# A streaming-encoder layer: two of the four sums of the first modulation as one-row TensorE products, and V's first rounding on ScalarE

## The chip, the core and the metric

One core of a Trainium2 chip runs the whole layer as one program. The metric is the device time of that program in microseconds (us); the median of three runs of the kernel before is 1326.62 us. The engines are called by their short names: PE (TensorE), DVE (VectorE), ACT (ScalarE), POOL (GpSimd) and SP (SyncE, which here only issues transfers).

## What is computed

The layer takes x (1024 rows of 1024 values) and a conditioning vector c of 1024 values. What matters here is the beginning of the reference:

```
mod = jnp.dot(jax.nn.silu(c), w_ada[l]) + b_ada[l]
sh_a, sc_a, g_a, sh_m, sc_m, g_m = jnp.split(mod, N_MOD, axis=-1)
h = modulate(rmsnorm(x, g_attn_norm[l]), sh_a, sc_a)
proj = jnp.dot(h, w_in[l])
```

`modulate` is h * (1 + scale) + shift. Everything behind it (two kinds of attention, the output projection, a gated MLP) starts from `proj`, and so from the shift and the scale, each of them 1024 sums over the 1024 values of silu(c).

## The kernel before, in words

The channels are cut into eight blocks of 128 (number d, 0 to 7), which lie on the 128 partitions; x has eight row tiles x0 to x7 of 128 rows, and h = 0 or 1 names the first or second four of them.

**The modulation.** The weights of scale and shift are packed in four blocks (dd, 0 to 3). One block serves two channel blocks d, has 512 columns, and is loaded in four chunks of 512 KB (`adaw`, L209), each with two of the eight groups k of 128 input channels. There are five chunk buffers, so that a chunk of the next block is loaded when one of the last block has been used. `ada_pair(dd)` (L271) makes the sums on DVE: one `tensor_scalar` (L276) and seven `scalar_tensor_tensor` (L278), all 128 x 512, add k's weights times silu(c) into `adacc`. This leaves 128 partial sums for each column, one for each partition; PE adds them up with a vector of ones (`p_ada`, L293), which puts the 128 columns on 128 partitions. Three short DVE instructions (L296 to L298) then make the two columns of `modT` for this d, scale and shift.

**x.** SP loads x0 to x7 behind the four chunks of block 0. For each tile ACT squares it and sums the squares (L224), POOL makes the reciprocal root (L119, L120), and DVE multiplies the tile by it (L226).

**The stage around the change.** For each d PE transposes the eight 128 x 128 pieces of x (`ht_ps`, L233), four for each h. ACT (h = 0 and the rounded half of h = 1, L236, L239) and DVE (h = 1, L241) apply scale and shift on the way out of PSUM. Each product is computed with split operands: a rounded part (hi) and the rest (lo, L242 on POOL for h = 0 and on DVE for h = 1), and three matmuls of 256 columns (L154 hi x hi, L155 hi x lo, L156 lo x hi). So `qk` takes 24 matmuls for each d, 192 in all. The weights of `qk` are split too (L77 on ACT, L84 on POOL). From d = 4 on, two pieces of V's weights are split for each d (`wv0_split`, L261): the rounding by `hi_of` on DVE (L81), the rest on POOL (L84), and a sum of squares on DVE (L267).

**What sets the order.** The order in which the instructions stand on each engine is made by a scheduler with a timing model when the program is built; each engine then runs its list strictly in that order, and so does SP with its transfers. The code asks in some places that one instruction comes after another (`issue_after`).

Of the kernel before, what the change touches and what calls it, by code (L numbers as in the profile page):

```python
# [13 lines left out]
F32 = mybir.dt.float32  # L14
# [4 lines left out]
AF = mybir.ActivationFunctionType  # L19
# [5 lines left out]
P = 128  # L25
# [3 lines left out]
ND = D // P  # L29
# [35 lines left out]
def layer_kernel(ctx, tc, I, out):  # L65
    nc = tc.nc
    pe, act, dve, pool, sp = nc.tensor, nc.scalar, nc.vector, nc.gpsimd, nc.sync
# [7 lines left out]
    def hi_of(eng, o, i):  # L75
        if eng == "a":
            act.activation(o, i, AF.Copy)  # L77
        elif eng == "p":
            pool.tensor_scalar(o, i, 1.0, 0.0, op0=MUL, op1=ADD)
        else:  # L80
            dve.tensor_copy(o, i)  # L81

    def lo_of(eng, o, i, hi):
        (pool if eng == "p" else dve).tensor_tensor(o, i, f32(hi), op=SUB)  # L84
# [15 lines left out]
    ones = cst.tile([P, P], F32, name="ones")  # L100
# [4 lines left out]
    cs = cst.tile([P, ND], F32, name="cs")  # L105
# [28 lines left out]
    ps = psA.__enter__()  # L134
# [3 lines left out]
    def rtile(name, shape=(P, 512), dt=F32):  # L138
        return apg.tile(list(shape), dt, name=name, tag="R", bufs=4)
# [10 lines left out]
    def gemm3(pt, pairs, start=True, stop=True):  # L150

        n = len(pairs)
        for i, (sh, sl, mh, ml) in enumerate(pairs):
            pe.matmul(pt, sh, mh, start=(start and i == 0), stop=False)  # L154
            pe.matmul(pt, sh, ml, start=False, stop=False)  # L155
            last = pe.matmul(pt, sl, mh, start=False, stop=(stop and i == n - 1))  # L156
        anchor["pe"] = last.ins
# [47 lines left out]
    wada = {}  # L205

    def load_ada(dd, c):
        w = st.tile([P, 2, 512], F32, name=f"adaw_{dd}_{c}", tag="wa", bufs=5)
        anchor["ada"] = sp.dma_start(w[:], I["w_ada_a"][dd][:, 2 * c:2 * c + 2]).ins  # L209
        wada[dd, c] = w  # L210
# [18 lines left out]
    def mod_transpose(src, k, h, row, pspool, psum_tag, pb, hpool, tag, tmp, nbuf, veng, leng):  # L229

        pt = pspool.tile([P, 512], F32, name=f"ht_ps{row}_{k}_{h}", tag=psum_tag, bufs=pb)
        for j in range(4):
            pe.transpose(pt[:, j * P:(j + 1) * P], src(j), ident[:])  # L233
        pg = hpool.tile([P, 2, 512], F32R, name=f"hT{row}_{k}_{h}", tag=tag, bufs=nbuf)
        a, b = modT[:, row, k:k + 1], modT[:, row + 1, k:k + 1]
        anchor["act"] = act.activation(pg[:, 0], pt[:], AF.Identity, scale=a, bias=b).ins  # L236
        v = tmp.tile([P, 512], F32, name=f"hv{row}_{k}_{h}", tag="hv", bufs=2)
        if veng == "a":
            act.activation(v[:], pt[:], AF.Identity, scale=a, bias=b)  # L239
        else:  # L240
            dve.tensor_scalar(v[:], pt[:], a, b, op0=MUL, op1=ADD)  # L241
        lo = (dve if leng == "v" else pool).tensor_tensor(pg[:, 1], v[:], f32(pg[:, 0]), op=SUB)  # L242
        anchor["lo" + leng] = lo.ins
        return pg
# [4 lines left out]
    accs = {}  # L249
    ssw0 = cst.tile([P, ND], F32, name="ssw0")  # L250

    wv0, wv0r = [], []

    def wv0_load():
        with tc.issue_after(anchor["ada"]):
            for k in range(ND):
                r = st.tile([P, 256], F32, name=f"wv0_r{k}", tag="wvr", bufs=8)
                anchor["sp"] = sp.dma_start(r[:], I["w_v"][0][:, k, :]).ins
                wv0r.append(r)

    def wv0_split(k):  # L261
        w = hw.tile([P, 2, 256], F32R, name=f"wv0_s{k}", tag="ws", bufs=16)
        junk = st.tile([P, 512], F32, name=f"wv0_j{k}", tag="wvj", bufs=1)
        with tc.issue_after(anchor["lov"]), tc.issue_after(anchor["lop"]):
            hi_of("v", w[:, 0], wv0r[k][:])
            lo_of("p", w[:, 1], wv0r[k][:], w[:, 0])
            dve.tensor_tensor_reduce(junk[:, :256], wv0r[k][:], wv0r[k][:], 1.0, 0.0, MUL, ADD,  # L267
                                     accum_out=ssw0[:, k:k + 1])
        wv0.append((w[:, 0], w[:, 1]))

    def ada_pair(dd):  # L271
        acc = rtile(f"adacc_{dd}")
        for k in range(ND):
            w = wada[dd, k // 2][:, k % 2]
            if k == 0:
                dve.tensor_scalar(acc[:], w, cs[:, 0:1], None, op0=MUL)  # L276
            else:
                dve.scalar_tensor_tensor(acc[:], w, cs[:, k:k + 1], acc[:], op0=MUL, op1=ADD)  # L278
        accs[dd] = acc

    ada_pair(0)
    for d in range(ND):
        dd, half = divmod(d, 2)
        if half == 0 and dd + 1 < ND // 2:
            for c in range(4):
                load_ada(dd + 1, c)
            if dd + 2 == ND // 2:
                wv0_load()
            ada_pair(dd + 1)
        pt = ps.tile([P, 512], F32, name=f"p_ada{d}", tag="mm", bufs=2)  # L290
        for i in range(2):
            c0 = half * 256 + i * P
            pe.matmul(pt[:, i:i + 1], accs[dd][:, c0:c0 + P], ones[:, 0:1], start=True, stop=True)  # L293

        tmp = cst.tile([P, 1], F32, name=f"adat{d}", tag="adat", bufs=2)
        dve.tensor_scalar(tmp[:], pt[:, 0:1], pk[:, C_B + 8 + d:C_B + 9 + d], 1.0, op0=ADD, op1=ADD)  # L296
        dve.tensor_tensor(modT[:, 0, d:d + 1], tmp[:], pk[:, C_GA + d:C_GA + d + 1], op=MUL)
        dve.tensor_tensor(modT[:, 1, d:d + 1], pt[:, 1:2], pk[:, C_B + d:C_B + d + 1], op=ADD)  # L298
        for h in range(2):
            hT[d, h] = mod_transpose(lambda j: xs[4 * h + j][:, d * P:(d + 1) * P], d, h, 0, ps, ("T", "pv")[h], 1,  # L300
                                     hw, "hT", st, 16, "v" if h else "a", "v" if h else "p")
        if d >= ND // 2:
            for k in range(2 * d - ND, 2 * d - ND + 2):
                wv0_split(k)
        for t in range(NT):
            h, j = divmod(t, 4)
            sl = slice(j * P, (j + 1) * P)
            gemm3(qk0[h][:, j * 256:(j + 1) * 256],
                  [(hT[d, h][:, 0, sl], hT[d, h][:, 1, sl]) + wqk[d]], start=(d == 0 and j % 2 == 0), stop=(d == ND - 1 and j % 2 == 1))
# [717 lines left out]
    for n in range(len(tiles) + DEPTH):  # L1027
        if n < len(tiles):
            u, i = tiles[n]
# [3 lines left out]
            if i % 4 == 2 and n + 2 < len(tiles):  # L1033
                v = tiles[n + 2][0]
# [4 lines left out]
        if n >= DEPTH:  # L1039
            u, i = tiles[n - DEPTH]  # L1040
# [66 lines left out]
    def mt(tag, shape, name, dt=F32):  # L1107
        return mp["a" if tag in ("raw", "w2", "ws") else "b"].tile(list(shape), dt, name=name, tag=tag, bufs=MB[tag])
# [72 lines left out]
    for t in range(NT):  # L1181
        pt = ps2.tile([P, 1024], F32, name=f"op{t}", tag="op", bufs=3)
# [69 lines left out]
    c0 = mt("c", [P, 4, 512], "c0")  # L1252
# [385 lines left out]
def build(arrays):  # L1638
    nc = bacc.Bacc("TRN2", target_bir_lowering=False, num_devices=1, dynamic_dma_scratch_size=1024)
    I = {k: nc.dram_tensor(k, v.shape, mybir.dt.from_np(v.dtype), kind="ExternalInput").ap()  # L1640
         for k, v in arrays.items()}
    out = nc.dram_tensor("out_0_dram", (S, D), F32, kind="ExternalOutput").ap()
    with tile.TileContext(nc, schedule_with_timeline_sim=True) as tc, ExitStack() as ctx:
        layer_kernel(ctx, tc, I, out)
    return nc
# [8 lines left out]
```

## Time and profile before

| | us |
|---|---|
| three runs | 1329.13, 1322.44, 1326.62 |
| the profiled execution | 1326.91 |
| its span, first to last instruction | 1325.1 |
| PE, DVE, ACT, POOL busy in the span | 1191.0, 1086.5, 623.6, 580.7 |

The profiled execution took 1.8 us more than its span. Times in the views are microseconds from the span's start. A row of a timeline gives start, duration, engine, line, operation, the tiles written and read, the count, and in brackets how long the engine stood idle before it and what released it. The matmuls of a run overlap, so that the distance from start to start tells their rate, not their duration.

### The profile page before, as it was taken

The page shows a single profiled execution, that of the slowest core. Times are in us where ns is not written, and L with a number is a line of the kernel's source. Part 1 is how long each engine was busy: PE and PEld are TensorE (multiplying, and loading weights), DVE is VectorE, ACT ScalarE, POOL GpSimd, SP SyncE. Part 2 cuts the span into 40 slices and gives each one's busy share as a digit, 9 for nine tenths or more (in the row PEclk, how much of TensorE's full clock was granted, in tenths as well). Part 3 has the DMA queues.
Part 4 walks back from the last instruction along what each step waited for, and adds up shares of the span by engine and source line. Part 5 has one row for each costly group of instructions (what it writes and reads, how often), then busy time and mean ns, then how long its engine had stood idle before and what let it go on. Part 6 is the DMA issues. An engine that isn't in the chain of part 4 may idle for free.

```text
span 1325.1 us, 18721 instructions
## 1 busy us (share of the span) xinstructions
PE 1191.0 (90%) x6168; PEld 992.2 (75%) x6168; DVE 1086.5 (82%) x1928; ACT 623.6 (47%) x1132; POOL 580.7 (44%) x613
## 2 busy tenths in 40 slices
PE   3899899888678788878899999999999998999998
PEld 3789888878556577756677888888888886888886
DVE  6979989887699978774789888888889886687667
ACT  5454654364556444452476444443444444433331
POOL 5485773586567643344515445454444431000000
PEclk9899899999879898888999999999999998999999
DMA  8416769665124677679602333333243336943441
GB/s 323 144 55 149 169 146 198 154 166 121 28 80 80 150 162 140 139 153 324 260 16 80 127 104 133 114 109 126 94 133 104 128 103 243 394 135 116 128 160 63
DMA packets 223689, 190.57 MB, mean 144 GB/s; under 512 B 148708, under 2 KB 166884, under 8 KB 223592
## 3 DMA queue, kind: packets, MB, share of 16 engines
q1 hardware_dynamic: 223592, 189.38, 49.9%
q8 instruction: 48, 0.79, 0.2%
q14 instruction: 49, 0.40, 0.1%
HBM read 117.24 MB, written 37.49 MB: 117 GB/s over the span
## 4 chain that ended last, share of the span: by engine, by line
PE 50%; DVE 4%; DMA 3%; issue 2%; ACT 1%; POOL 1%; SPq 0%; POOLq 0%; DVEq 0%; ACTq 0%
PE p L1130 10%; PE p L1131 10%; PE p L1132 10%; PE dnA_P L1465 2%; PE dnA_P L1467 2%; PE dnA_P L1466 2%; DMA PTm<-hlm 2%; PE dnB_P L1467 2%; PE dnB_P L1465 2%; PE dnB_P L1466 2%; PE dnA L1465 1%; PE dnA L1466 1%; PE dnA L1467 1%; PE sm L803 1%; PE dnB L1467 1%
## 5 line engine op out<-in xcount | busy, mean ns | idle before, releaser
L77 ACT ACTIVATE dnP<-dnr 128x1024 fp32r<-128x1024 f32 x73 | 77.5, 1064 | 117.3 <-PE dnA_P L1467 46.3
L1439 DVE TENSOR_TENSOR dnP<-dnr,dnP 128x1024 fp32r<-128x1024 f32 x72 | 87.9, 1223 | 52.7 <-ACT dnP L77 52.7
L73 POOL TENSOR_SCALAR hlm<-Pm,rim 128x512 f16<-128x512 f32 (+2 forms) x96 | 68.8, 728 | 85.7 <-DVE rim L832 45.6
L84 POOL TENSOR_TENSOR wf<-wu,wf 128x512 fp32r<-128x512 f32 x22 | 38.7, 1758 | 116.2 <-ACT wf L77 116.2
L84 POOL TENSOR_TENSOR wb<-wu,wb 128x512 fp32r<-128x512 f32 x22 | 44.7, 2033 | 84.9 <-ACT wb L77 57.1
L1301 DVE SCALAR_TENSOR_TENSOR u<-c,cvp,u 128x1023 f32<-128x1023 f32 x44 | 55.8, 1309 | 27.8 <-ACT u L1300 23.7
L891 PE MATMUL pvm<-PTm,vt 128*128 128x256 f16 (+1 forms) x320 | 47.9, 302 | 27.1 <-DMA PTm<-hlm 27.0
L851 DVE SCALAR_TENSOR_TENSOR hlm<-Pm,rim,hlm 128x512 f16<-128x512 f32 (+2 forms) x96 | 66.3, 708 | 6.0 <-POOL hlm L73 5.8
L73 POOL TENSOR_SCALAR hlc<-Pc,ric 128x640 f16<-128x640 f32 (+2 forms) x64 | 48.8, 764 | 47.0 <-DVE ric L832 17.8
L829 ACT ACTIVATE Pc<-sc,mc 128x640 f32<-128x640 f32 (+2 forms) x64 | 42.2, 660 | 54.9 <-DVE mc L818 36.9
L891 PEld LDWEIGHTS <-vt 128*128 128x128 f16 x320 | 32.9, 111 | 42.3 <-issue 21.2
L829 ACT ACTIVATE Pm<-sm,mm 128x128 f32<-128x128 f32 (+3 forms) x64 | 47.2, 738 | 35.1 <-DVE sm L821 9.7
L1300 ACT ACTIVATE u<-c,cvp 128x1024 f32<-128x1024 f32 x44 | 52.3, 1238 | 23.6 <-DVE c L1399 16.5
L77 ACT ACTIVATE wc<-ws 128x512 fp32r<-128x512 f32 x21 | 13.3, 632 | 92.9 <-DVE ws L1149 87.1
L851 DVE SCALAR_TENSOR_TENSOR hlc<-Pc,ric,hlc 128x640 f16<-128x640 f32 (+2 forms) x64 | 50.9, 801 | 7.0 <-POOL hlc L73 6.8
L154 PE MATMUL ipq<-wq_s,hT 128*128 128x256 f32 x192 | 56.2, 293 | 0.0
L1302 DVE SCALAR_TENSOR_TENSOR u<-c,cvp,u 128x1022 f32<-128x1022 f32 x44 | 55.5, 1300 | 0.0
L155 PE MATMUL ipq<-wq_s,hT 128*128 128x256 f32 x192 | 55.0, 286 | 0.0
L156 PE MATMUL ipq<-wq_s,hT 128*128 128x256 f32 x192 | 54.9, 286 | 0.0
L1466 PE MATMUL dnA_P<-dnP 128*128 128x512 f32 x132 | 51.3, 389 | 0.0
L1467 PE MATMUL dnA_P<-dnP 128*128 128x512 f32 x132 | 51.3, 389 | 0.0
L1465 PE MATMUL dnA_P<-dnP 128*128 128x512 f32 x132 | 51.2, 389 | 0.0
(443 smaller groups left out, 4399.7 us busy)
## 6 DMA issues: line engine op xcount, KB each, us to landing
wu<-w_up SPq DMA_DIRECT2D x44, 512.0 KB, 3.5
dnr<-g_d SPq DMA_DIRECT2D x73, 256.0 KB, 2.7
aw<-w_ada SPq DMA_DIRECT2D x48, 256.0 KB, 3.3
g_d<-u SPq DMA_DIRECT2D x22, 512.0 KB, 2.8
dnr<-w_down SPq DMA_DIRECT2D x44, 256.0 KB, 5.4
adaw<-w_ada_a SPq DMA_DIRECT2D x16, 512.0 KB, 6.4
x<-x SPq DMA_DIRECT2D x16, 512.0 KB, 9.0
g_d<-gs SPq DMA_DIRECT2D x22, 256.0 KB, 2.7
```

The costliest lines, as they stand in the source:

```text
L73: pool.tensor_scalar(o, i, s, 1.0, op0=MUL, op1=MUL)
L77: act.activation(o, i, AF.Copy)
L84: (pool if eng == "p" else dve).tensor_tensor(o, i, f32(hi), op=SUB)
L829: act.activation(pr[:, :n], sv, AF.Exp, bias=m[:], scale=-1.0, accum_out=rsum[:, 0:1])
L851: dve.scalar_tensor_tensor(hl[:, w:2 * w], pp, ri[:], hl[:, :w], op0=MUL, op1=SUB)
L1130: pe.matmul(pt, sh, pg[:, 0], start=(k == 0 and not add), stop=False, skip_group_check=skip)
L1131: pe.matmul(pt, sh, pg[:, 1], start=False, stop=False, skip_group_check=skip)
L1132: last = pe.matmul(pt, sl, pg[:, 0], start=False, stop=(k == 3), skip_group_check=skip)
L1439: r = f(*a, **k)
L1465: pe.matmul(pt, sh, w[:, 0, 0], start=start, stop=False, skip_group_check=add)
L1466: pe.matmul(pt, sh, w[:, 1, 0], start=False, stop=False, skip_group_check=add)
L1467: pe.matmul(pt, sl, w[:, 0, 0], start=False, stop=stop, skip_group_check=add)
```

## The change

Blocks 0 and 1 (channel blocks d = 0 to 3) are no longer summed by DVE. Instead PE takes one column of silu(c) as the stationary operand and streams the 512 columns of the weights as they were loaded, in float32, eight products into one row of PSUM (`p_row`, L276 of the changed kernel). ACT copies the row to SBUF (L277), and the sums are put on partitions by the same `p_ada` products as before, now with one row instead of 128. Blocks 2 and 3 stay on DVE. The rounding of V's first weights goes from DVE to ACT.

```
-            hi_of("v", w[:, 0], wv0r[k][:])
+            hi_of("a", w[:, 0], wv0r[k][:])
...
         acc = rtile(f"adacc_{dd}")
+        if dd in (0, 1):
+            pr = ps.tile([P, 512], F32, name=f"p_row{dd}", tag="mm", bufs=2)
+            for k in range(ND):
+                pe.matmul(pr[0:1, :], cs[:, k:k + 1], wada[dd, k // 2][:, k % 2], start=(k == 0), stop=(k == ND - 1))
+            act.activation(acc[0:1, :], pr[0:1, :], AF.Copy)
+            accs[dd] = acc[0:1, :]
+            return
...
-            pe.matmul(pt[:, i:i + 1], accs[dd][:, c0:c0 + P], ones[:, 0:1], start=True, stop=True)
+            src = accs[dd][:, c0:c0 + P]
+            pe.matmul(pt[:, i:i + 1], src, ones[:src.shape[0], 0:1], start=True, stop=True)
```

The lines behind it move down by seven or eight in the changed kernel. The scheduler also puts rows elsewhere. On ACT, at the start of the program (`xj` is the square of an x tile, `p_row_212` the row of block 0), the list before is:

```order
L224 ACTIVATE xj_128,ssx<-x_112 128x1024
L224 ACTIVATE xj_133,ssx<-x_114 128x1024
L224 ACTIVATE xj_138,ssx<-x_116 128x1024
L224 ACTIVATE xj_143,ssx<-x_118 128x1024
L224 ACTIVATE xj_148,ssx<-x_120 128x1024
L224 ACTIVATE xj_153,ssx<-x_122 128x1024
L236 ACTIVATE hT_0_0_249<-ht_ps_0_0_244,modT 128x512
```

and now, with x0 to x7 as x_112, x_114 and so on to x_126:

```order
L224 ACTIVATE xj_128,ssx<-x_112 128x1024
L224 ACTIVATE xj_133,ssx<-x_114 128x1024
L277 ACTIVATE adacc_211<-p_row_212 1x512
L224 ACTIVATE xj_138,ssx<-x_116 128x1024
L224 ACTIVATE xj_143,ssx<-x_118 128x1024
```

The copy of block 0's row stands ahead of the squares of x2 to x7, and hT of d = 0, h = 0 has moved behind all of them.

On PE, behind the transposes of x0 to x5 for d = 0, the list before goes on with the last two transposes of d = 0, those of d = 1 and the first `qk`:

```order
L233 MATMUL ht_ps_0_1_254<-ident,x_124 128x128
L233 MATMUL ht_ps_1_0_295<-ident,x_112 128x128
L233 MATMUL ht_ps_1_0_295<-ident,x_114 128x128
L233 MATMUL ht_ps_1_0_295<-ident,x_116 128x128
L233 MATMUL ht_ps_1_0_295<-ident,x_118 128x128
L154 MATMUL qk_0_208<-wq_s_168,hT_0_0_249 128x256
L233 MATMUL ht_ps_0_1_254<-ident,x_126 128x128
```

and now (`p_row_231` is block 1's row, `p_ada_241` and `p_ada_292` belong to d = 0 and d = 1; "x2" is two products):

```order
L233 MATMUL ht_ps_0_1_258<-ident,x_124 128x128
L276 MATMUL p_row_231<-adaw_0_222,cs 1x512 x2
L301 MATMUL p_ada_241<-ones,adacc_211 128x1 x2
L233 MATMUL ht_ps_0_1_258<-ident,x_126 128x128
L276 MATMUL p_row_231<-adaw_1_224,cs 1x512 x2
L276 MATMUL p_row_231<-adaw_2_226,cs 1x512 x2
L276 MATMUL p_row_231<-adaw_3_228,cs 1x512 x2
L301 MATMUL p_ada_292<-ones,adacc_211 128x1 x2
L154 MATMUL qk_0_208<-wq_s_168,hT_0_0_253 128x256
```

All eight products of block 1 and both `p_ada` pairs of block 0 now stand between the transpose of x6 and the first `qk`; block 0's eight products stand at the head of PE's list, ahead of every transpose.

On DVE, behind the scaling of x7, the changed list is (`adacc_351` is block 2, `adacc_486` block 3):

```order
L226 TENSOR_SCALAR x_126<-x_126,rx 128x1024
L304 TENSOR_SCALAR adat_244<-p_ada_241,pk 128x1
L306 TENSOR_TENSOR modT<-p_ada_241,pk 128x1
L305 TENSOR_TENSOR modT<-adat_244,pk 128x1
L241 TENSOR_SCALAR hv_0_1_265<-ht_ps_0_1_258,modT 128x512
L242 TENSOR_TENSOR hT_0_1_263<-hv_0_1_265,hT_0_1_263 128x512
L283 TENSOR_SCALAR adacc_351<-adaw_0_343,cs 128x512
L304 TENSOR_SCALAR adat_295<-p_ada_292,pk 128x1
L306 TENSOR_TENSOR modT<-p_ada_292,pk 128x1
L285 SCALAR_TENSOR_TENSOR adacc_351<-adaw_0_343,cs,adacc_351 128x512
```

Before, the `modT` columns of d = 0 and 1 stood ahead of most of the scaling, and block 1's sums stood where block 2's stand now. Behind this stage the lists of all engines are the same for a long stretch. They differ again in the attention stages: on SP from the second load of `bias` behind it, which the profile of before has at 211 us, up to the last x tiles, at about 640 us. Behind those they are the same to the end, but for line numbers.

More of the change, by code (lines that the diff above doesn't have):

```diff
@@ L278, in ada_pair @@
                 dve.scalar_tensor_tensor(acc[:], w, cs[:, k:k + 1], acc[:], op0=MUL, op1=ADD)
-        accs[dd] = acc
+        accs[dd] = acc[:, :]
     ada_pair(0)
```

## The prediction

> **What bounds the kernel now.** The chain of waits, in order of time, begins with this piece:
>
> ```profile
> 496.24 0.02 issue
> ```
>
> It reaches back only to 496 us, so it says nothing of the place of the change. I read the table of busy time by stage first, with stretches cut at the events of the first stage. Its columns are the stretch, its length, and busy time (with the number of instructions) of PE, PE's weight loads, DVE, ACT and POOL, then PE's granted clock, DMA share and GB/s.
>
> ```profile
> 6.50:12.50 6.00, 0.00 (x0) 0.00 (x0) 5.75 (x8) 0.96 (x1) 0.00 (x0) 1.00 1.02 413
> 12.50:26.40 13.90, 6.71 (x21) 4.31 (x21) 8.30 (x15) 10.40 (x22) 11.66 (x19) 1.00 1.03 404
> 26.40:40.40 14.00, 10.42 (x67) 9.34 (x67) 13.82 (x24) 4.74 (x9) 6.54 (x6) 0.97 0.71 217
> 40.40:56.00 15.60, 14.32 (x93) 13.42 (x94) 15.53 (x28) 7.86 (x12) 7.94 (x6) 0.80 0.63 202
> 56.00:70.70 14.70, 12.56 (x102) 11.71 (x100) 14.60 (x37) 5.17 (x8) 8.74 (x10) 1.00 0.01 2
> 95.00:125.00 30.00, 30.00 (x247) 29.20 (x246) 28.78 (x94) 13.99 (x33) 14.82 (x18) 1.00 0.50 119
> 200.00:640.00 440.00, 359.86 (x2035) 296.52 (x2036) 351.40 (x911) 218.41 (x514) 242.95 (x317) 0.91 0.64 152
> ```
>
> Up to 26 us DMA runs at its full share and PE has little to do. From 26.4 to 70.7 us DVE is busy for 43.95 of 44.3 us, PE for 37.3: DVE limits this stage, as the change supposes, but PE is only 7 us behind it. From 95 to 125 us PE is busy without a gap, so a few microseconds won or lost before are not made up there. Next, the waits of this stage:
>
> ```profile
> PE p_ada L293 <- DVE adacc L278: 12.6, 1, 12.6
> ACT hT L236 <- DVE modT L297: 12.7, 3, 6.7
> ```
>
> PE stands idle for 12.6 us before block 0's sums, and ACT waits 12.7 us in three pieces for the later ones. Idle time at the start is free for PE work only if nothing queued behind that work is late.
>
> **What the change takes off.**
>
> ```profile
> 6.50 0.49 DVE L276 TENSOR_SCALAR adacc<-adaw,cs 128x512 f32<-128x512 f32 x1 [3.28 <-DMA adaw<-w_ada_a]
> 7.02 5.47 DVE L278 SCALAR_TENSOR_TENSOR adacc<-adaw,cs,adacc 128x512 f32<-128x512 f32 x7
> 24.06 1.75 DVE L226 TENSOR_SCALAR x<-x,rx 128x1024 f32<-128x1024 f32 x1 [0.72 <-POOL rx L120]
> 31.16 3.03 DVE L278 SCALAR_TENSOR_TENSOR adacc<-adaw,cs,adacc 128x512 f32<-128x512 f32 x3
> 39.48 2.31 DVE L278 SCALAR_TENSOR_TENSOR adacc<-adaw,cs,adacc 128x512 f32<-128x512 f32 x3
> 55.41 1.36 DVE L81 CAST wv_s<-wv_r 128x256 fp32r<-128x256 f32 x1
> 60.45 0.28 DVE L81 CAST wv_s<-wv_r 128x256 fp32r<-128x256 f32 x1
> ```
>
> Block 0's sums lie before 12.5 us, where DVE waits for x afterwards anyway: worth nothing on DVE. Block 1's eight cost 0.77 to 1.01 us each (2.31 and 3.03 by three), 6 to 8 us. The eight casts cost 0.28 to 1.36 us each, say 5 us. So DVE is relieved of some 12 of its 44 us. On ACT, busy for 17.8 of 44.3 us, the eight casts are hidden.
>
> **What it adds, walked through.** First the prices on PE:
>
> ```profile
> 142.08 1.91 PE L486 MATMUL p_ada<-aacc,ones 128*128 128x512 f32 x2
> 172.97 1.10 PE L486 MATMUL p_ada<-aacc,ones 128*128 128x512 f32 x2 [0.20 <-DVE aacc L485]
> 24.38 0.56 PE L154 MATMUL qk<-wq_s,hT 128*128 128x256 f32 x1
> 28.54 0.41 PE L155 MATMUL qk<-wq_s,hT 128*128 128x256 f32 x1
> 28.75 0.41 PE L156 MATMUL qk<-wq_s,hT 128*128 128x256 f32 x1
> 29.53 0.28 PE L155 MATMUL qk<-wq_s,hT 128*128 128x256 f32 x1
> 31.75 0.28 PE L156 MATMUL qk<-wq_s,hT 128*128 128x256 f32 x1
> 31.87 0.28 PE L154 MATMUL qk<-wq_s,hT 128*128 128x256 f32 x1
> ```
>
> L486 is the nearest row: a float32 product of 512 columns, in two instructions. It took 1.91 us once and 1.10 us another time; less about 0.2 us of drain, which the next product covers, I take 1.75 us slow and 0.9 us fast. The same two speeds appear in the `qk` rows, 0.21 us from start to start before about 29.5 us and 0.12 after, though the granted clock stands at 1.00. The trace has no product with a one-column stationary operand; its price I bound by slow and fast.
>
> By the Trainium skill, page "TensorE: Matmul & The Clock Gate", section "Part 1: The HAM clock gate (the "warmup" mystery)", PE's clock is halved until about 3.4 us of sustained work, in a window that runs freely. By that rule block 0's row would end between 15.2 and 16.9 us, an estimate around the value that I take below.
>
> Here `qk` went fast 5.1 us after its first matmul, from 24.38 to 29.53, so I let PE go fast about 5 us after it starts. Block 0's products start when the first chunk is there, at 6.50 where DVE began: three slow, five fast, 6.5 + 5.25 + 4.5 = 16.3 us. ACT then copies the row (0.60 us by the copy of a 128x512 PSUM tile) to 16.9. Behind this copy in ACT's list stand the squares of x2 to x7:
>
> ```profile
> 14.17 1.06 ACT L224 ACTIVATE xj<-x 128x1024 bf16<-128x1024 f32 x1 [0.20 <-DMA x<-x]
> 72.15 0.60 ACT L349 ACTIVATE raw<-qk 128x512 f32<-128x512 f32 x1
> 16.71 0.75 DVE L226 TENSOR_SCALAR x<-x,rx 128x1024 f32<-128x1024 f32 x1 [0.72 <-POOL rx L120]
> 18.18 0.75 DVE L226 TENSOR_SCALAR x<-x,rx 128x1024 f32<-128x1024 f32 x1 [0.72 <-POOL rx L120]
> ```
>
> x2's square started at 14.17, when its data arrived; now it starts at 16.9, 2.7 us later. From there the tiles follow at 1.47 us (16.71 to 18.18), a loop of POOL's root and DVE's scaling that ACT does not set, so nothing is caught up: x7's scaling goes from 24.06 to 26.8, x6's ends at 26.1. That is the **first cost**, 2.7 us, bounded by 1.6 (16.3 less 1.1 for a clock that rises at once after two products) and 6.9 (all eight slow).
>
> PE transposes x6 until 26.7. By then it has done only scattered transposes for 10 us, so it is slow again, as `qk` was at 24.4. Now block 1's products, which stand ahead of `qk`: two slow ones to 30.2, four instructions of `p_ada` to 31.1 (0.23 each), x7's transpose, then six products, fast by then, to 37.0, and two more pairs of `p_ada`:
>
> ```profile
> 12.64 1.84 PE L293 MATMUL p_ada<-ones,adacc 128*128 128x1 f32 x8 [12.64 <-DVE adacc L278]
> 36.49 1.05 PE L293 MATMUL p_ada<-ones,adacc 128*128 128x1 f32 x8
> 26.45 0.58 PE L155 MATMUL qk<-wq_s,hT 128*128 128x256 f32 x1
> 29.73 1.09 PE L233 MATMUL ht_ps<-ident,x 128*128 128x128 f32 x8
> 71.54 0.28 PE L156 MATMUL qk<-wq_s,hT 128*128 128x256 f32 x1
> ```
>
> The first `qk` comes at 37.5, where before it ran steadily from 26.45. This is the **second cost**: DVE's sums of block 1 ran beside `qk`, PE's stand in its way. What is left for PE then: 192 `qk` at 0.12 us, 23.0; 56 transposes at 1.09 for eight, 7.6; six groups of `p_ada`, 1.05 for two, 3.2. Sum 33.8 us: not before 71.3. Before, the last `qk` started at 71.54 and ended at 71.8.
>
> Then the waits that remain. scale and shift of d = 2 come from block 1. Behind `modT` of d = 1 (38.0 us) DVE's list has seven sums (0.77 to 1.01 each), a 0.7 us scaling and short ones before `modT` of d = 2: 44.6 to 46.3, and ACT's hT 0.8 us later. PE, with 38 `qk`, twelve transposes and two groups of `p_ada` (4.6 + 1.6 + 1.1) in between, is there at 44.8: it waits 0.6 to 2.3 us, I take 1.5. After that DVE, with 15 sums where it had 24, keeps ahead; I keep 1 us for the other waits, since the 56.0:70.70 row still had 2.1 us without PE work. So the last `qk` ends at 71.3 + 1.5 + 1 = 73.8, **2.0 us later** than before. The 1.4 us at the end that the casts took from POOL's second parts is in none of PE's waits.
>
> **The sum.** 12 us off DVE; on PE 14.5 to 28 us of products, of which 10 lie in idle time and the others delay x by 2.7 us and the first `qk` by 11 us; PE's slack eats 9 of these 11. Net +2 us on the profiled execution's 1326.9, which lies 0.3 us above the median of the three runs: 1329 us. About 0.5%, 6.6 us, is what a measurement of this kernel can tell from no change; this is inside.
>
> **The rivals.** (A) *The one-row products stay slow.* They use one column of the array. If that does not raise the clock, block 0 ends at 6.5 + 14 = 20.5, x7's scaling starts at 31.0, block 1's products end at 46, and `qk` begins slow at 46.4: + 33.8 + 2 for five slow microseconds = 82.2, that is 10.5 us later, 1337 us. It decides from about six products in eight slow. For it speaks that the transposes of the first tiles left PE slow at 24.4; against it that these were apart, with PE busy for 6.71 of 13.9 us, and that block 0's products follow without gaps.
>
> The same page, section "Part 4: PE-mode transpose", says that transposes do not count as busy work for the clock. It says nothing of a one-column operand; if these counted as little, rival A would follow. The slow start at 24.4 us agrees with it as to transposes; no row here shows the other.
>
> (B) *PE pays less than I count.* If the clock rises early in both rows, block 0 ends at 15.2 and the first `qk` starts at 35, and with DVE relieved only 0.5 us of waiting remains: 35 + 33.8 + 0.5 = 69.3, 2.5 us earlier, 1324 us. Against it speaks that PE's windows before show both speeds again at 40 to 46 us.
>
> (C) *The attention's order decides.* Between about 211 and 640 us the lists differ without any work being changed. There PE waits, by the table, 80 us:
>
> ```profile
> PE pvm L891 <- DMA PTm<-hlm: 27.0, 16, 4.8
> PE sm L803 <- ACT Pm L829: 12.2, 13, 2.2
> ```
>
> The sixteen waits for transposed tiles cost 1.7 us each on average. Four of them more or fewer are 7 us, which is my price for a reshuffle, to 1336 or 1322; all of the 27 us would be the end of the range, and nothing names a direction. That the change does not do what it says can be left out: the lists show the products on PE and the casts on ACT.
>
> **How the numbers follow.** My forecast 0.46 (its own range 1324 to 1334), A 0.22, B 0.12, C 0.20, half on each side. Slower by over 0.5%: A nearly whole (0.20), half of C (0.10), the forecast's upper end (0.04), 0.34. Faster: half of C (0.10) and the ends of B (0.03), 0.13. Within: 0.53. The range goes from 1319 (C downwards, from B) to 1338 (A).
>
> **What would show it.** In the changed profile ACT's copy at L277 should end near 17 us and x2's square follow it at once; x7's scaling should start near 26.8 us; the first `qk` should come near 37.5 us and the last end near 74. One-row products 0.85 us apart per instruction throughout, or L277 after 20 us, mean A; a first `qk` before 35.5 us means B; a last `qk` in time and another end means C. I am wrong as to the mechanism if ACT waits nowhere at L277, or if DVE is still busy without a gap from 38 to 70 us.

## The result, and the profile after

The changed kernel took 1331.01 us in the median of 12 runs (1323.02 to 1335.86), the kernel before 1326.45 us in 12 runs: a ratio of 1.0044, with a 95% interval of 1.0026 to 1.0062, or 3.4 to 8.2 us more. The forecast was 1329 us, in a range of 1319 to 1338. The profiled execution took 1335.86 us (span 1334.0), the longest of the twelve; its parts are read with that in mind, and a second profile of the same kernel follows in the experiments.

The first stage, by the table of busy time in the stretches of the prediction (same columns):

```profile
6.50:12.50 6.00, 6.00 (x10) 0.88 (x8) 0.00 (x0) 1.14 (x2) 0.00 (x0) 1.00 1.02 401
12.50:26.40 13.90, 6.63 (x17) 1.82 (x16) 6.05 (x8) 8.90 (x19) 9.63 (x18) 0.81 1.02 402
26.40:40.40 14.00, 14.00 (x66) 7.28 (x64) 8.04 (x14) 6.47 (x12) 8.73 (x9) 0.94 0.73 224
40.40:56.00 15.60, 12.38 (x67) 11.79 (x67) 12.84 (x30) 6.50 (x14) 2.80 (x2) 0.67 0.60 199
56.00:70.70 14.70, 14.70 (x129) 14.70 (x128) 12.68 (x27) 8.24 (x12) 8.43 (x9) 1.00 0.01 2
```

From 26.4 to 70.7 us DVE is busy for 33.56 us where it was 43.95, and PE for 41.08 where it was 37.3: the limit went over from DVE to PE, as the change supposes. But from 40.4 to 56.0 us PE idles for 3.2 us, and its granted clock is 0.67 where it was 0.80. The timeline of the same stage, PE, ACT and DVE:

```profile
6.41 9.25 PE L276 MATMUL p_row<-adaw,cs 128*1 128x512 f32 x16 [6.41 <-DMA adaw<-w_ada_a]
15.70 0.59 ACT L277 ACTIVATE adacc<-p_row 1x512 f32<-1x512 f32 x1 [1.91 <-PE p_row L276]
25.62 1.21 DVE L226 TENSOR_SCALAR x<-x,rx 128x1024 f32<-128x1024 f32 x1 [0.72 <-POOL rx L120]
25.37 3.16 PE L276 MATMUL p_row<-adaw,cs 128*1 128x512 f32 x4
29.26 5.31 PE L276 MATMUL p_row<-adaw,cs 128*1 128x512 f32 x12
35.03 0.39 PE L154 MATMUL qk<-wq_s,hT 128*128 128x256 f32 x1
42.26 0.28 PE L155 MATMUL qk<-wq_s,hT 128*128 128x256 f32 x1
42.28 0.49 DVE L283 TENSOR_SCALAR adacc<-adaw,cs 128x512 f32<-128x512 f32 x1 [2.58 <-DMA adaw<-w_ada_a]
43.34 0.21 DVE L304 TENSOR_SCALAR adat<-p_ada,pk 128x1 f32<-128x1 f32 x1
45.15 1.09 PE L233 MATMUL ht_ps<-ident,x 128*128 128x128 f32 x4 [2.61 <-DVE adat L304]
46.85 0.58 PE L154 MATMUL qk<-wq_s,hT 128*128 128x256 f32 x1 [0.61 <-ACT hT L236]
47.23 0.41 PE L155 MATMUL qk<-wq_s,hT 128*128 128x256 f32 x1
75.76 0.28 PE L156 MATMUL qk<-wq_s,hT 128*128 128x256 f32 x1
```

The reader sees block 0's row ahead of everything, ACT waiting for it with x2's square queued behind its copy, and x7's scaling at 25.62 instead of 24.06. Block 1's twelve last instructions take 0.44 us each (5.31 by 12), and the first `qk` starts at 35.03. Then comes what the forecast had too small: DVE waits 2.58 us for the first chunk of block 3 (L283), and the `adat` of d = 2 stands behind that in its list. PE has no `qk` from 42.54 to 46.85, and those behind the gap start 0.21 us apart (46.85 and 47.23 are the first pair) until 54.5, where they had been 0.12 apart. The last `qk` starts at 75.76, 4.2 us later than before.

In the attention, where nothing but the order was changed, the same table and PE's waits between 200 and 640 us (total, times, longest) give:

```profile
200.00:640.00 440.00, 360.67 (x2022) 298.06 (x2022) 351.37 (x918) 215.29 (x511) 236.66 (x311) 0.88 0.63 144
PE pvm L899 <- DMA PTm<-hlm: 20.9, 11, 6.8
PE pvc L899 <- DMA PTc<-hlc: 11.7, 8, 5.6
```

Eleven waits for `PTm` where there were sixteen, but longer ones; 11.7 us of waits for `PTc` where there were 5.5; and a clock of 0.88 for 0.91. The first transpose of the second modulation, the first row behind the attention, starts at 648.32 us, where it was 640.42: of 7.9 us at that point, 4.2 are there already at the last `qk`.

### The profile page after: what moved, and what is told of

Same layout as the page of the kernel before. It is cut to its first block, busy times and chain, and to the rows that moved or that the text cites. A ratio compares the mean times of both kernels' runs of the same rounds, so it can differ in the third digit from the quotient of the medians.

```text
span 1334.0 us, 18740 instructions
## 1 busy us (share of the span) xinstructions
PE 1212.0 (91%) x6200; PEld 998.4 (75%) x6200; DVE 1088.9 (82%) x1904; ACT 623.8 (47%) x1142; POOL 574.6 (43%) x613
## 4 chain that ended last, share of the span: by engine, by line
PE 32%; DVE 18%; issue 6%; DMA 5%; ACT 3%; POOL 2%; SPq 0%; DVEq 0%; ACTq 0%; POOLq 0%
PE p L1138 3%; PE p L1140 3%; PE p L1139 3%; DVE u L1310 3%; DVE u L1309 2%; PE dnA_P L1473 2%; PE dnA_P L1474 2%; PE dnA_P L1475 2%; PE dnB_P L1473 1%; PE dnB_P L1474 1%; PE dnB_P L1475 1%; ACT u L1308 1%; DMA PTm<-hlm 1%; DVE hlm L859 1%; DVE we L84 1%
## 5 line engine op out<-in xcount | busy, mean ns | idle before, releaser
L73 POOL TENSOR_SCALAR hlm<-Pm,rim 128x512 f16<-128x512 f32 (+3 forms) x96 | 70.6, 746 | 80.0 <-DVE rim L840 20.9
L1309 DVE SCALAR_TENSOR_TENSOR u<-c,cvp,u 128x1023 f32<-128x1023 f32 x44 | 65.9, 1538 | 27.6 <-ACT u L1308 27.6
L859 DVE SCALAR_TENSOR_TENSOR hlm<-Pm,rim,hlm 128x512 f16<-128x512 f32 (+3 forms) x96 | 67.8, 719 | 7.3 <-POOL hlm L73 6.6
L1310 DVE SCALAR_TENSOR_TENSOR u<-c,cvp,u 128x1022 f32<-128x1022 f32 x44 | 66.8, 1557 | 0.0
L84 POOL TENSOR_TENSOR wb<-wu,wb 128x512 fp32r<-128x512 f32 x22 | 38.8, 1765 | 58.1 <-ACT wb L77 55.9
L899 PE MATMUL pvc<-PTc,v 128*128 128x256 f16 (+1 forms) x288 | 36.9, 275 | 17.6 <-DMA PTc<-hlc 15.1
L1474 PE MATMUL dnA_P<-dnP 128*128 128x512 f32 x132 | 51.3, 389 | 0.0
L1475 PE MATMUL dnA_P<-dnP 128*128 128x512 f32 x132 | 51.3, 389 | 0.0
```

Source lines behind the costliest of these rows:

```text
L73: pool.tensor_scalar(o, i, s, 1.0, op0=MUL, op1=MUL)
L859: dve.scalar_tensor_tensor(hl[:, w:2 * w], pp, ri[:], hl[:, :w], op0=MUL, op1=SUB)
L899: last = pe.matmul(dst, u.vst(j), mov, start=(x == 0), stop=(x == len(todo) - 1), skip_group_check=True)
L1309: dve.scalar_tensor_tensor(u[:, 1:], c[:, :S - 1], cvp[:, cv + 1:cv + 2], u[:, 1:], op0=MUL, op1=ADD)
L1310: dve.scalar_tensor_tensor(u[:, 2:], c[:, :S - 2], cvp[:, cv:cv + 1], u[:, 2:], op0=MUL, op1=ADD)
L1474: pe.matmul(pt, sh, w[:, 1, 0], start=False, stop=False, skip_group_check=add)
```

## Experiments

Each kernel ran in five rounds beside the kernel before. The time to before is the ratio less 1, times before's 1325.5 us; "rest" is that time less what its profile shows at the last `qk`. Lines behind an edit stand one or two further down than in the changed kernel. "List" says which order of the attention the kernel has: two kernels with one letter have the same rows there on every engine.

| kernel | list | last qk, us | to before | ratio, 95% interval | time to before | rest |
|---|---|---|---|---|---|---|
| before | B | 71.54 | 0 | 1 | 0 | 0 |
| six of V's roundings on ACT | B | 69.41 | -2.1 | 0.9984 [0.9969, 0.9999] | -2.1 | 0.0 |
| before, late x | B | 73.26 | +1.7 | 1.0025 [1.0008, 1.0043] | +3.3 | +1.6 |
| changed | A | 75.76 | +4.2 | 1.0044 [1.0026, 1.0062] | +5.8 | +1.6 |
| changed, again | A | 73.68 | +2.1 | 1.0043 [1.0027, 1.0059] | +5.7 | +3.6 |
| copy behind the squares | A | 72.76 | +1.2 | 1.0017 [1.0006, 1.0029] | +2.3 | +1.1 |
| V and block 1's row | A | 72.30 | +0.8 | 0.9998 [0.9980, 1.0016] | -0.3 | -1.1 |
| the same, late x | A | 75.34 | +3.8 | 1.0020 [1.0004, 1.0036] | +2.7 | -1.1 |
| V alone | V | 70.14 | -1.4 | 1.0083 [1.0058, 1.0109] | +11.0 | +12.4 |
| V and block 0's row | V | 72.46 | +0.9 | 1.0054 [1.0034, 1.0074] | +7.2 | +6.3 |
| V alone, late x | V | 72.00 | +0.5 | 1.0080 [1.0051, 1.0109] | +10.6 | +10.1 |
| two more products | N | 71.05 | -0.5 | 1.0042 [1.0023, 1.0061] | +5.6 | +6.1 |
| block 3 late | K | 73.50 | +2.0 | 1.0031 [1.0019, 1.0043] | +4.1 | +2.1 |
| qk first | Q | 77.57 | +6.0 | 1.0020 [1.0003, 1.0037] | +2.7 | -3.4 |

The intervals are 1.5 to 4 us wide on either side, and a last `qk` is that of one execution, so a rest under some 4 us says little.

### The changed kernel again

No edit.

> The changed kernel once more, unchanged, beside the three others on the same chip: the ratio should again be 1.0026 to 1.0062. How far its profile repeats the first one's landmarks (last qk 75.8, last ipq 261.4, first transpose of the second modulation 648.3) says how much of a difference of two profiles is chance: theory, the start stage repeats within 0.3 us and the attention within 2 us; rival, the attention alone varies by 5 us from one execution to the next.

Measured: the ratio repeats, 1.0043. The first stage does not, in the timeline of PE:

```profile
6.23 8.49 PE L276 MATMUL p_row<-adaw,cs 128*1 128x512 f32 x16 [6.23 <-DMA adaw<-w_ada_a]
29.28 7.20 PE L276 MATMUL p_row<-adaw,cs 128*1 128x512 f32 x12
44.18 0.28 PE L155 MATMUL qk<-wq_s,hT 128*128 128x256 f32 x1
45.31 0.63 PE L233 MATMUL ht_ps<-ident,x 128*128 128x128 f32 x4 [0.85 <-DVE adat L304]
47.01 0.39 PE L154 MATMUL qk<-wq_s,hT 128*128 128x256 f32 x1 [1.07 <-ACT hT L236]
47.23 0.28 PE L155 MATMUL qk<-wq_s,hT 128*128 128x256 f32 x1
73.68 0.28 PE L156 MATMUL qk<-wq_s,hT 128*128 128x256 f32 x1
```

Block 0's row took 8.49 us for 9.25, block 1's twelve instructions 7.20 for 5.31, and the first `qk` came at 36.94 for 35.03. Yet the last came 2.1 us earlier: PE reached the gap later, the gap was 2.55 us for 4.31, and behind it the `qk` stayed 0.12 us apart. So the theory fell, and the rival holds as to the attention alone: the first stage varies by 2 us too, by PE's clock, and from the last `ipq` (261.4 and 263.7 us) to the first transpose of the second modulation (648.3 and 645.6) the attention differs by 5 us. A stage of one profile is known to some 2 us, and no better.

### The parts alone

V's rounding alone is `hi_of("v", ...)` to `hi_of("a", ...)` at L265 of the kernel before; block 0 alone and block 1 alone are the changed kernel with `if dd in (0,):` and `if dd in (1,):` at L273.

> Before, with V's first rounding on ACT and no row products. Theory 1 (the start stage costs some 4 us through the row products, the rest of the change is the order of the attention): the last qk stays at 71 to 72 us, since ACT has 26 us free in that stage and the casts were in none of PE's waits; the whole time then differs from before only by what the new attention order is worth, -5 to +5 us. Theory 2 (the casts on ACT hold up hT): last qk 73 us or later. Theory 3 (a shorter DVE list pays here): last qk 70.5 us or earlier and the whole time lower by as much.

> V's rounding on ACT and only block 0 by row products; block 1 is summed by DVE as before. Its lists equal those of the kernel with the rounding alone, but for block 0's own rows at the start, so the difference of the two is block 0's price with the attention order held. Theory 1: the first squares of x start 2 us later, x7's scaling 1.5 us later (25.6 for 24.06), and since DVE is busy to the end of the stage the last qk is 1 to 1.6 us later, and so is the whole time (1.0008 to 1.0012 of the other). Theory 2 (the start has slack): last qk and time equal within 0.3 us. Theory 3 (the warm clock pays): last qk earlier by 0.5 us or more.

> V's rounding on ACT and only block 1 by row products; block 0 is summed by DVE as before. Its lists equal those of the changed kernel, attention included, but for block 0's own rows. Theory 1: without the late squares x7's scaling is back near 24.1 us, the first qk near 33.5, the last qk 1 to 1.6 us earlier than the 75.8 of the changed kernel, so still 2.5 to 3.3 us later than before, and the whole time 1.5 us below the changed kernel's, about +4.5 us on before. Theory 2 (what PE waits for at d = 2 is the transfer of block 3's first chunk, whatever comes ahead): the last qk stays at 75.8 and the time at +6. Theory 3 (nearly all of the loss is block 0's late x): last qk within 0.5 us of before's 71.5.

Measured: V alone has its last `qk` at 70.14, 1.4 us earlier than before, which is the first half of theory 3; the second half, a whole time lower by as much, did not come: it is 11 us longer. Its attention, from the last `ipq` to the second modulation, against that of before:

```profile
257.40:640.40 383.00, 306.99 (x1606) 246.22 (x1606) 300.60 (x770) 192.50 (x452) 217.31 (x284) 0.90 0.62 149
```

```profile
256.40:654.40 398.00, 313.05 (x1608) 250.39 (x1607) 303.01 (x770) 191.88 (x451) 212.88 (x283) 0.88 0.60 146
```

The same work takes 15 us longer: PE is busy for 6 us more at a lower granted clock, and idles for 85 us instead of 76. This order alone costs more than the seven microseconds at which I had put any order.

Block 0's row on top of it moves the last `qk` from 70.14 to 72.46, 2.3 us. That is more than the 1 to 1.6 of theory 1, and the whole time went down, by 3.8 us, with intervals that overlap; that no theory had. Block 1's row with V's rounding ends the stage at 72.30, where theory 1 had 74.2 to 74.8, and takes before's time. That is nearest to its theory 3, that block 0 makes nearly all of the loss, and 0.3 us outside what that had. Its gap:

```profile
28.29 6.80 PE L276 MATMUL p_row<-adaw,cs 128*1 128x512 f32 x12
42.72 0.28 PE L155 MATMUL qk<-wq_s,hT 128*128 128x256 f32 x1
45.64 0.38 PE L154 MATMUL qk<-wq_s,hT 128*128 128x256 f32 x1 [1.07 <-ACT hT L236]
72.30 0.28 PE L156 MATMUL qk<-wq_s,hT 128*128 128x256 f32 x1
```

A gap of 2.64 us, and the clock stays. Since the lists are those of the changed kernel, block 0's row costs 6 us there (1.0044 less 0.9998), give or take 3.4.

### The first cost: the copy ahead of the squares

```diff
-            act.activation(acc[0:1, :], pr[0:1, :], AF.Copy)
+            with tc.issue_after(anchor["sq"]):
+                act.activation(acc[0:1, :], pr[0:1, :], AF.Copy)
```

(`anchor["sq"]` is set to the latest square of x at L224.)

> The changed kernel with one row moved: ACT's copy of block 0's row stands behind the eight squares of x, not ahead of the last six. All other lists are word for word those of the changed kernel, attention included. Theory 1 (this copy delays x): the squares start at 14.2 again, x7's scaling at about 24.0 where it was 25.6, and block 1's products and the first qk 1.6 us earlier (33.4). The gap of PE at d = 2 then shrinks by less than that, since the transfer of block 3's first chunk ends it; if the gap falls to 3 us or less PE stays fast behind it, and the last qk comes at 72 to 73 instead of 75.8. Rival (the x tiles have slack): x7 earlier and the last qk within 0.5 us of 75.8. Whole time: by the sum of the stages 3 us below the changed kernel (1.002 of before); if the attention answers in steps to when it begins, anything from 0.998 to 1.006.

Measured, on DVE and PE:

```profile
23.61 1.20 DVE L226 TENSOR_SCALAR x<-x,rx 128x1024 f32<-128x1024 f32 x1 [0.72 <-POOL rx L120]
```

```profile
40.25 0.28 PE L155 MATMUL qk<-wq_s,hT 128*128 128x256 f32 x1
44.14 0.58 PE L154 MATMUL qk<-wq_s,hT 128*128 128x256 f32 x1 [1.07 <-ACT hT L236]
```

x7's scaling is back at 23.61, the first `qk` comes at 32.99, and the time falls from 1.0043 to 1.0017, by 3.4 us, give or take 2.6. Theory 1 holds as to the copy: it is about half of what the change costs. The gap is 3.61 us and PE slow behind it (0.21 us apart), so the last `qk` at 72.76 is what theory 1 had, but not by its way: against the first execution x7 and the first `qk` are both 2.0 us earlier, and the clock gained nothing.

Three kernels with a delay of x and nothing else test the same from the other side. x0 is squared three times instead of once, with the same output, so that ACT begins the next squares 2.5 us later:

```diff
-        act.activation(junk[:], xt[:], AF.Square, accum_out=ssx[:, t:t + 1])
+        for z in range(1 + 2 * (t == 0)):
+            act.activation(junk[:], xt[:], AF.Square, accum_out=ssx[:, t:t + 1])
```

> Before, with x0 squared three times on ACT instead of once, so that all squares behind it and x7's scaling come 2.5 us later; every list else is that of before. Theory 1 (x sets the first stage, and the attention passes a delay on): last qk 73 to 74, last ipq 259 to 260, whole time +2 to +2.5 us, 1.0015 to 1.002. Rival A (the first stage has slack behind x): all landmarks within 0.5 us of before and the time 1.000. Rival B (the attention answers in its own way): the last qk late by 2 and the whole time anywhere from -4 to +6.

> Block 1 by row products and V's rounding on ACT, as in the earlier run that matched before's time, with x0 squared three times: all squares come 2.5 us later, and all lists else stay those of the changed kernel without block 0's row. Theory 1 (block 0's row costs what it costs by delaying x, and this attention order passes the delay on or widens it): last qk 74 to 75.5, whole time 2.5 to 6 us above before, 1.002 to 1.0045. Rival (block 0's row costs through its products on PE, not through x): the time stays within 1.5 us of before, 1.000 to 1.001.

> V's rounding on ACT with x0 squared three times: all squares 2.5 us later, all lists else those of the kernel with the rounding alone, which was 1.0083 of before, and those of the one with block 0's row, which was 1.0054 although its first stage ended 2.3 us later. Theory 1 (on this order of the attention a later start happens to pay): the time falls to 1.005 to 1.0065 of before. Rival (a delay adds up, and block 0's row helped in another way): 1.009 to 1.011.

Measured, x7's scaling in before with late x, and the gap in the kernel with block 1's row and late x:

```profile
26.11 1.75 DVE L227 TENSOR_SCALAR x<-x,rx 128x1024 f32<-128x1024 f32 x1 [0.71 <-POOL rx L120]
```

```profile
29.77 5.31 PE L277 MATMUL p_row<-adaw,cs 128*1 128x512 f32 x12
42.69 0.28 PE L155 MATMUL qk<-wq_s,hT 128*128 128x256 f32 x1
46.57 0.58 PE L154 MATMUL qk<-wq_s,hT 128*128 128x256 f32 x1 [1.07 <-ACT hT L237]
```

With x7 2.05 us later, before's last `qk` is 1.7 us later and its time 3.3 us longer (interval 1.1 to 5.7). With block 1's row, 2.3 us on x7 are 3.0 us on the last `qk` and 2.9 us on the time. So on both lists a delay of x comes out at the end at about its size, as theory 1 has it. That the size fits so well is in part luck, since PE's clock differs too. In before PE's granted clock is 0.5 from 39.7 to 46.5 us, with late x only from 44.4 to 47.8. In the second kernel the delay does not go through the first `qk` (35.48, without the delay 35.49): block 1's products ran faster, and the delay came out in the gap of 3.60 us and in the slow `qk` behind it (a granted clock of 0.5 from 45.8 to 56.0 us, where it stayed at 1 without the delay). On V's list the last `qk` is 1.9 us later and the time the same within its 3 to 4 us: the interval holds both theories' ranges in part and decides neither, and whether and why block 0's row took less there is open.

### The second cost, and the gap at d = 2

Block 1's products behind the `qk` of d = 0 (the call of `ada_pair(1)` moved behind that loop, in `tc.issue_after(anchor["pe"])`):

> The changed kernel with block 1's eight products put behind the 24 qk of d = 0 instead of ahead of them. Theory 1 (the second cost is qk standing behind the products): the first qk comes near 27 instead of 35.0, and since scale and shift of d = 2 come some 3 us earlier than before relative to the work left, the last qk is 2 to 4 us earlier than 75.8. Rival (PE's work is the same and only its order changes, so nothing is won; the waits for modT of d = 1 and 2 take the place): last qk 75 or later. The attention comes in another order too, up to 6 us either way on the whole time.

```profile
32.77 0.28 PE L156 MATMUL qk<-wq_s,hT 128*128 128x256 f32 x1
32.98 7.03 PE L276 MATMUL p_row<-adaw,cs 128*1 128x512 f32 x16
42.46 0.39 PE L154 MATMUL qk<-wq_s,hT 128*128 128x256 f32 x1 [0.72 <-ACT hT L236]
```

```profile
40.58 0.22 DVE L305 TENSOR_SCALAR adat<-p_ada,pk 128x1 f32<-128x1 f32 x1 [9.86 <-PE p_ada L302]
```

Theory 1 fell. The first `qk` comes at 25.98, and the last at 77.57. The products take 7.03 us here (8.47 and 10.77 in the two executions of the changed kernel), `p_ada` of d = 1 now stands behind them, and DVE waits 9.86 us for it with its sums queued behind: 9.4 us without `qk`. The rival had it: PE's work is the same and a wait takes the place. The whole time is 3 us below the changed kernel's nonetheless, on an order of its own and with intervals that overlap.

Then the sums of block 3 held back on DVE:

```diff
-            ada_pair(dd + 1)
+            with tc.issue_after(anchor["modT"]) if dd == 2 else contextlib.nullcontext():
+                ada_pair(dd + 1)
```

(`anchor["modT"]` is the latest shift column of `modT`.)

> The changed kernel with DVE's sums of block 3 held behind the modT columns of d = 3; they stood ahead of those of d = 2, and DVE waited 2.6 us for their first chunk. Theory 1 (this order on DVE makes PE's gap at d = 2, and the gap makes the next 24 qk slow): adat of d = 2 comes at about 40.6 instead of 43.3, PE's gap between the qk at 42.26 and 46.85 falls below 2 us, the qk behind it stay 0.12 us apart, and the last qk comes at 71.5 to 73. Rival (block 3's chunk is late for everything behind it too): the gap moves to d = 6 and the last qk stays within 1 us of 75.8. The attention's rows come in another order as well, so the whole time may move by up to 6 us either way against what this stage gives.

```profile
43.09 0.20 DVE L305 TENSOR_SCALAR adat<-p_ada,pk 128x1 f32<-128x1 f32 x1
45.21 0.47 DVE L283 TENSOR_SCALAR adacc<-adaw,cs 128x512 f32<-128x512 f32 x1
```

```profile
44.83 0.28 PE L155 MATMUL qk<-wq_s,hT 128*128 128x256 f32 x1
46.02 0.39 PE L154 MATMUL qk<-wq_s,hT 128*128 128x256 f32 x1 [0.22 <-ACT hT L236]
```

`adat` of d = 2 no longer waits for the chunk (it comes at 43.09, not at 40.6, since the first `qk` is 2.6 us late), the gap is 0.91 us, and PE stays fast. From the first `qk` (37.59) to the last (73.50) it takes 35.9 us, where the two executions of the changed kernel took 40.7 and 36.7. Theory 1 holds as to the gap; the last `qk` missed its 73 by half a microsecond, since block 1's products happened to be slow (37.59 for 35.03).

### The order of the attention

Two more products: L293 of before issued a second time for d = 7, into columns that nobody reads.

> Before, with two more one-column products (a second copy of d = 7's pair of p_ada, written to columns that nobody reads) at the end of the first stage: 0.25 to 0.5 us more work on PE. The lists of all engines stay those of before up to about 200 us, and the attention's rows come in another order. Theory of the order: the whole time moves by more than the 0.5 us, up to 5 us either way, and the landmarks up to 200 us do not. Rival: the attention's order is worth nothing, and the time is +0.3 us, 1.0002.

Six of V's eight roundings on ACT:

```diff
-            hi_of("v", w[:, 0], wv0r[k][:])
+            hi_of("v" if k in (4, 6) else "a", w[:, 0], wv0r[k][:])
```

> Before, with six of V's eight first roundings on ACT and the other two (k = 4 and 6) on DVE. With this split the attention's lists on all engines stay word for word those of before. Theory 1 (the roundings on ACT win a little in the first stage, and the 12 us that all eight cost came from the attention's new order alone): last qk at 70.1 to 71.0 where before had 71.5, and the whole time 0 to 1.5 us below before, 0.999 to 1.000. Rival (the roundings on ACT do harm by themselves): the time 4 us or more above before, 1.003. This is also the one part of the change that could beat both kernels.

Measured: half a microsecond of added work that leaves the last `qk` at 71.05 makes the kernel 5.6 us slower, on another order. The six roundings, on before's order, make it 2.1 us faster, by an interval of 0.1 to 4.1, and the last `qk` is earlier by the same 2.1. POOL's second parts waited for the roundings, before and with six of them on ACT, between 40 and 72 us:

```profile
POOL wv_s L84 <- DVE wv_s L81: 6.2, 7, 2.3
```

```profile
POOL wv_s L84 <- DVE wv_s L81: 2.0, 2, 1.8
```

The theory of the order holds in both, a little beyond its bounds: 5.6 us where it had at most 5, and with six roundings 69.41 and 2.1 us where it had at least 70.1 and at most 1.5. The kernel with six roundings is the only one here that beats before clear of the noise, if narrowly.

## Why the prediction was right, and where it was not

**Block 0's row: right, somewhat too dear.** I let it end at 16.3 and ACT's copy at 16.9; they ended at 15.66 and 16.29, and in the second execution at 14.72 and 15.35. x7's scaling moved to 25.62 and 24.69, not 26.8: 1.6 and 0.6 us, with 1.6 my lower bound, so the second lies under it. The mechanism is shown by the late copy, and a delay of x does reach the end, at about its size by one pair of profiles on each list. A product is 0.88 us fast, and I had 0.9.

**Block 1's products ahead of `qk`: right.** I had the first `qk` at 37.5, and it came at 35.03 and 36.94. PE's work from there, 33.8 us plus 2.5 of waits, is 36.3 to the end of the last `qk`; it was 37.0 where the clock stayed up, and 41.0 in the first execution, where it fell.

**The wait at d = 2: mis-sized.** I took 1.5 us out of a range of 0.6 to 2.3, from DVE's seven sums. I did not see that one of these sums needs block 3's first chunk, which takes the buffer of block 1's last chunk and so cannot be fetched before PE's last product; it was used 6.8 us after its issue at 35.48 us. The wait is 3.2 us in the first execution (2.61 and 0.61) and 1.9 in the second, and in the first it is followed by 24 `qk` at half speed, 2.2 us more. The early first `qk` of that execution was lost again here. That is why the last `qk` was at +4.2 there, and at +2.1, beside my +2.0, in the other. This agreement is in part luck: my sum had all `qk` fast, as they were in the second execution, but before, from which I counted, has 16 of them at half speed (40.41 to 45.49 us).

**V's roundings: the step that failed.** I put the gain from them at nothing, since POOL's second parts were in none of PE's waits. In the profile of before they were in one, under another name:

```profile
65.97 0.86 POOL L84 TENSOR_TENSOR wv_s<-wv_r,wv_s 128x256 fp32r<-128x256 f32 x1 [2.30 <-DVE wv_s L81]
67.85 1.26 POOL L242 TENSOR_TENSOR hT<-hv,hT 128x512 fp32r<-128x512 f32 x1
69.16 0.39 PE L156 MATMUL qk<-wq_s,hT 128*128 128x256 f32 x1 [1.50 <-POOL hT L242]
```

A second part waits 2.30 us for the rounding on DVE, the low half of hT stands two rows behind it in POOL's list, and PE waits 1.50 us for that. With all eight roundings on ACT the wait at this place is 0.33 us:

```profile
68.97 0.38 PE L156 MATMUL qk<-wq_s,hT 128*128 128x256 f32 x1 [0.33 <-DVE hT L242]
```

The last `qk` is 1.4 us earlier with all eight and 2.1 us with six, by one profile each, and with six the whole time followed. Part of this stood before any rounding. Counted from the first `qk` behind the group of transposes and `p_ada` at 46.9 to 49.8 us (47.77 in before), the last `qk` comes 23.8 to 24.1 us later in three kernels with the roundings on DVE (before, before with late x, two more products), 22.7 to 23.2 in three with all on ACT (V alone, V alone with late x, V and block 0's row) and 22.2 with six. So the roundings were worth about 1 us (eight) and 1.7 us (six), the two row products cost the stage some 3 to 5 us and not 2, and V's part gave some of it back.

**The rivals.** Products that stay slow (A) did not come: 0.44 us for an instruction in 5.31 by 12, and PE fast behind them in the first `qk`. B did not either, though the first `qk` in the first execution came before its 35.5. C, the attention's order, I priced at 7 us either way. An order can be worth more: the rest is +6 to +12 on V's list and +6 with two more products; the -3 where `qk` goes first is within the scatter. The changed kernel's own order is nearly neutral: five runs on its list leave a rest of -1.1 to +3.6, 0.8 on average. So of its 5.8 us some 2 to 4 come from the first stage, by the products and the late x, and the rest is no more than that scatter.

**Open.** What in V's list makes the attention 6 to 12 us longer was not found; no single wait of PE in it grew by more than 3 us. Nor is it known why a later start there did no harm, or how much of the rest of 1.6 and 3.6 us in the two executions of the changed kernel is chance.

## What to carry to other kernels

Work given to an engine that waits is free only until the next row of its list is late: read what stands behind it, on the engine and on the buffers that it holds. Where a scheduler orders the rows, a change of one stage can reorder another, and here that was worth up to 12 us against 2 to 4 from the change itself; so compare kernels whose other lists are the same, and look for the version of an edit that leaves them so. Six roundings instead of eight did, and the whole time followed the first stage. And when a term is put at nothing because it is in nobody's waits, follow the list of the engine that waits for it: the row behind it may be in them.

## What the runs showed of the hardware

A float32 product with a one-column stationary operand and 512 streamed columns takes two instructions of 0.44 us (5.31 by 12) or 0.89 us (3.57 by 4, at the start of block 1 with block 1's row alone); the product with 128 columns at L486, by which I had priced it, gave 0.9 and 1.75 us for the two instructions, so the columns left out save about no time.

PE's speed behind a pause of `qk` goes with the length of the pause, but not with that alone. At d = 2, with block 1 as a row, the `qk` stayed 0.12 us apart after gaps of 0.91, 2.55 and 2.64 us; after 3.60, 3.61 and 4.31 us they were 0.21 apart for two dozen, and the four transposes within each gap did not keep the clock up. The Trainium skill, page "TensorE: Matmul & The Clock Gate", section "HAM oscillation — how this bites in real kernels", has idle gaps over about 3.4 us put the clock back; these six gaps agree, if the transposes are counted as idle. Before does not fit it so simply:

```profile
33.90 0.28 PE L155 MATMUL qk<-wq_s,hT 128*128 128x256 f32 x1
37.76 0.39 PE L156 MATMUL qk<-wq_s,hT 128*128 128x256 f32 x1 [0.21 <-DVE hT L242]
40.41 0.58 PE L154 MATMUL qk<-wq_s,hT 128*128 128x256 f32 x1 [1.19 <-ACT hT L236]
```

After 3.58 us without `qk`, with four transposes and eight instructions of `p_ada` in them, ten `qk` still ran 0.12 us apart; the granted clock fell to 0.5 only at 39.7 us, in an idle time of 1.19 us, and stayed there to 46.5. In V alone it fell four `qk` behind a gap of 3.23 us. So for gaps between about 3 and 3.6 us these traces do not say what decides. Row products do keep the clock up: with `qk` first, 9.41 us pass without `qk`, 7.03 of them full of block 1's products, and the granted clock stays at 1 through them and the first `qk` behind, until 45.2 us.

The Trainium skill, the same page, section "Part 1: The HAM clock gate (the "warmup" mystery)", lets the window run freely, so that a kernel's slow start varies; block 0's row, 9.25 and 8.49 us in two executions of one kernel, agrees, and block 1's twelve instructions, 5.31 and 7.20, vary in the same way.
